# Residual adds free both banks first, background visits go round three times, later DMA landings are assumed, and sample scores take four column tiles at a time

## The chip, the cores and the metric

The kernel runs on one core of a Trainium2 chip. The time is the device time of one execution in microseconds (us). Of before there are three timed runs: 2312.69, 2312.80 and 2317.56 us, median 2312.8 us. The profile is of one more execution, of 2314.36 us, whose span from the first to the last instruction is 2312.2 us.

Engines: PE is TensorE (matmuls), PEld its loading of weights, DVE is VectorE, ACT ScalarE, POOL GpSimd, SP SyncE (which issues most DMAs).

## What is computed

One inference step of a decoder with two layers over a prompt of 512 tokens and a sample group of 8 sequences of 8 tokens, 576 rows in all, with width 2048. Cut to what matters:

```python
def step(x_prompt, x_sample, cache_win_k, cache_win_v, ...):
    # layer 0: attention heads and gated convolution from one projection
    proj = rms_norm(x, g) @ w_in                 # 2048 -> 8 * 1024
    q, k, v, z_a, gate_b, gate_c, h_in, z_b = jnp.split(proj, 8, axis=-1)
    o_a = dilated_attn(q, k, v)                  # sample rows also read the cache, 8 sequences of 2048 keys
    o_b = gate_b * causal_short_conv(gate_c * h_in) * silu(z_b)
    x = x + concat(o_a * silu(z_a), o_b) @ w_out
    # layer 1: diagonal complex SSM, 128 groups of 16 channels and 64 states
    u, z = split(rms_norm(x, g1) @ w_in_c, 2)
    y = gelu(Re(C h(u)) + D * u)
    x = x + (half_glu(y) * silu(z)) @ w_out_c
    return rms_norm(x, g_final), new caches, new states
```

## The kernel before, in words

**Main work.** The projections are cut into 120 jobs: 0 to 23 the heads' q, k and v, 24 to 31 z_a, 32 to 63 the convolution, 64 to 67 the output projection of layer 0 ("wide" jobs of 512 columns), 68 to 99 u and z of layer 1, 100 to 115 the half GLU, 116 to 119 the output projection of layer 1 (wide). Each product is made of three matmuls in a rounded format: `a_hi` by `wh`, `a_lo` by `wh`, `a_hi` by `wl`, where ACT makes `wh` from the loaded weight `w` and DVE makes `wl`, the rest. Accumulators are `mm` tiles of two PSUM banks, of which there are two (four banks); a wide job uses two of them for the 512 prompt rows (column tiles of the result `i` = 0 to 3, tiles 0 and 1 in the first `mm`) and `mms` with `jp` for the 64 sample rows (`i` = 4). `mm_tile` (L595) hands out a new `mm` once all but one of those handed out before have been counted as evacuated in `mmc["ev"]`; before, `finished` (L590) counts when the whole evacuation generator has ended.

**Background work.** Everything else (attention, the loads of the cache, the preparation of layer 1's SSM matrices, the convolution, the scan, residual adds) is written as Python generators, "threads". Each yields `W(engine, tiles, slot=..., flag=...)`: what its next piece waits for. The kernel text is emitted by a planner that keeps an estimated clock for each engine (class `Clock`, L79): `cost` (L151) prices an instruction, `op` adds it to its engine, and a DMA's landing is estimated as the end of its transfer plus a constant (L183). Between the matmuls of the main jobs `between` (L600) calls `step` (L431), which moves every thread once whose wait is over by the estimate (`could`, L405, with a tolerance `EPSN` of 150 ns); evacuations (`cur`) are asked first. So the estimates set the order in which the instructions of each engine stand; at run time real semaphores rule.

**Places that the change touches.** (1) *Sample scores*, `sample_near` (L1428). For each of four pairs of sequences and four blocks of 128 near keys, the keys of one sequence are loaded (`kv`), transposed (`tkn`), copied to `KT` and multiplied: `sps<-KT,qz`, fp32 matmuls with 32 columns of weights, each in a column tile of the array given by `tile_position`. One visit to the scores serves one sequence, in two column tiles. The values follow as `os<-kv,PTs` in four column tiles; the far keys as `kf` on DVE. The kv tiles have 6 buffers, kf 3. (2) *Layer 1's preparation during the heads*: chunks of SSM matrices, whose inputs `E` and `B` are loaded from scratch (one buffer each) when the chunk before has read them; DVE makes `tb`, `X`, `Cs`, and TensorE `gp<-Cs,B`. (3) *Layer 1's scan*: u is written as `uu` to scratch (`u_scr`), loaded back as `U`, and used in `vps<-U`. (4) *Residual adds* `ev_out0` (L1584) and `ev_out1` (L2014): for each bank of an `mm`, DVE adds the residual (`h<-mm,xr` or `Y<-mm,Y`), then ACT squares the sum for the norm. (5) *The tail*, `finish` (L2030), which scales rows by the norm's factor and weights and stores them.

Of the kernel before, what the change touches and what calls it, by code (L numbers as in the profile page):

```python
# [78 lines left out]
class Clock:  # L79
# [71 lines left out]
    def cost(self, eng, op, outs, ins):  # L151
        n = max(int(np.prod(a.shape[1:])) for a in outs[:1] + ins)
        if eng == "PE":
            if op == "transpose":
                return 110.0
            m, k = int(np.prod(ins[0].shape[1:])), int(np.prod(ins[1].shape[1:]))
            if ins[0].dtype == F32R:
                return k / 2.4 + 11 if k < 300 else k / 2.4 + 3
            if m <= 32:
                return max(138.0, 0.55 * k)  # L160
            return 2 * max(109.0, k / 1.2 + 2)
        wide = any(len(a.ap) > 1 and abs(int(a.ap[-1][0])) > 1 for a in outs + ins)
        if eng == "ACT":
            return 175 + 0.89 * n + (190 if len(outs) > 1 else 0)
        if eng == "DVE":
            if op in ("tensor_copy", "tensor_scalar", "memset") and all(a.tensor.name in self.sbuf for a in ins):
                return 150 + n / 1.3
            return 150 + n / (0.6 if wide else 0.96)
        return 200 + (2.15 if op == "tensor_tensor" else 1.0) * n

    def op(self, eng, op, a, k):
        aps = [(n, x) for n, x in list(enumerate(a)) + list(k.items()) if hasattr(x, "tensor")]
        outs = [x for n, x in aps if n in (0, "out", "accum_out")]
        ins = [x for n, x in aps if n not in (0, "out", "accum_out")]
        by = "DMA" if op == "dma_start" else eng
        t = max([self.when(x, False, by) for x in ins] + [self.when(x, True, by) for x in outs])
        if op == "dma_start":
            at = max(self.t[eng], t) + 370
            self.t[eng] = at
            n = int(np.prod(outs[0].shape))  # L180
            run = min(self.packets(x, x.tensor.name in self.row) for x in outs + ins)
            self.dma = max(self.dma, at) + n / run * (5 + 0.2 * run) / 16
            end = max(self.dma, at) + 1900  # L183
        else:
            at = max(self.t[eng], t + 60)
            two = op != "memset" and sum(x.tensor.name in self.sbuf for x in ins) > 1
# [92 lines left out]
def hybrid_step(tc, I, O):  # L279
# [122 lines left out]
    def now():  # L402
        return clk.t["PE"]

    def could(th, deep):  # L405
# [9 lines left out]
        return at <= lim + EPSN  # L415

    def next_evac():
        while evq and not cur:
# [4 lines left out]
    def run(th):  # L423
        if not advance(th):
# [3 lines left out]
            else:  # L428
                bg.remove(th)

    def step():  # L431
        next_evac()
        while cur and could(cur[0], 9000.0):
            run(cur[0])
        for th in list(bg):
            if th in bg and could(th, 3500.0):
                run(th)
                while cur and could(cur[0], 9000.0):
                    run(cur[0])

    def force():
        next_evac()
# [147 lines left out]
    def finished(g, tiles=1, jobs_=1):  # L590
        yield from g
        mmc["ev"] += tiles
        cnt["done"] += jobs_

    def mm_tile():  # L595
        until(lambda: mmc["ev"] > mmc["al"] - 2)
        mmc["al"] += 1
# [12 lines left out]
    def run_wide(n, hook, need):  # L610
        j = jobs[n]
        x, last = wide(j["x"]())
        acc = {}
        evac = lambda part, tiles, done: evq.append(finished(j["evac"](part, j["n"], acc), tiles, done))

        def mms(k, i):
            if k == 0 and i in (0, 2):
# [23 lines left out]
                    mms(k, t)  # L641
            release(n, k)
        i = cnt["i"]
        for t in range(5):
            for k in range(s, 16):
                if (k - s) % 2 == 0:
                    hook(n, k)
# [2 lines left out]
                must(i + k - s)  # L650
                mms(k, t)
            if s < 14:
                evac(t, 1 if t in (1, 3) else 0, 1 if t == 4 else 0)
            elif t in (1, 3, 4):
                evac(t, 1 if t < 4 else 0, 1 if t == 4 else 0)
        for k in range(s, 16):
# [736 lines left out]
                sa["fs"][b // 2] = fs  # L1393

    def sample_out(pr, osb):
        yield W("PE", osb, slot=[bgs()])
# [31 lines left out]
    def sample_near():  # L1428
# [3 lines left out]
        for pr in range(4):  # L1432
# [13 lines left out]
            prev = None  # L1446
            sps = None
            for t in range(4):
                for b2 in range(2):
# [13 lines left out]
                    kts[t, b2] = kk  # L1463
                    at += 1
                    sa["used"] = at
                    if prev:
                        yield W("PE", kts[prev], sa["qz"], slot=[] if sps is not None else [(pm, "bgl", 1)])
                        if sps is None:
                            sps = bgl_tile([P, 4, P], "sps")
                        scores(*prev)  # L1470
                    prev = (t, b2)
            yield W("PE", kts[prev], slot=[bgs(), (pp, "Ss", 1)])
            scores(*prev)
# [107 lines left out]

    h1 = {"x": {}, "xc": 0, "h": {}, "tg": 0, "an": 0, "t": {}, "sn": 0}

    def ev_out0(part, g, acc):  # L1584
        for i in ((0, 1), (2, 3), (4,))[part // 2]:
            n = P if i < 4 else 64
            yield W("DVE", flag=lambda: (g, i) in h1["x"] and (i == 4 or 4 * g + i - 4 * h1["tg"] < 6))
            x = h1["x"].pop((g, i))
            tag = "h" if i < 4 else "hs"
            ps = acc[i, 0]  # L1590
            if i == 4:
                ps = yield from joined(ps)
# [61 lines left out]
    def x_again():  # L1654
        yield W("SP", flag=lambda: "out" in h1)
        k = 0
        for g in range(4):
            for i in range(5):
                yield W("SP", slot=[(EV["p"], "xr", 1)], flag=lambda: k - h1["xc"] < 3)
# [354 lines left out]
    def ev_out1(part, g, acc):  # L2014
        for i in ((0, 1), (2, 3), (4,))[part // 2] if g < 3 else (part,):
            yield W("DVE", flag=lambda: fo.get("h", 0) > g)
            y = fo["Y"][:, i, g * 512:(g + 1) * 512] if i < 4 else fo["Ys"][:, g * 512:(g + 1) * 512]
            n = P if i < 4 else 64
            ps = acc[i, 0]
            if i == 4:  # L2020
                ps = yield from joined(ps)
            yield W("DVE", ps, y)
            add(y, ps, y)
            yield W("ACT", y)
            j = EV["p"].tile([P, 512], F32, name="junk2", tag="junk2", bufs=2)
            act(j[0:n], y, AF.Square, accum_out=ssqa[0:n, 4 * i + g:4 * i + g + 1])
            if g == 3:
                spawn(finish(i), prio=1)

    def finish(i):  # L2030

        n = P if i < 4 else 64
        v, r, w = [fo["s"][0:n, i, k:k + 1] for k in range(3)]
        sq = ssqa[0:n, 4 * i:4 * i + 4]
        yield W("DVE", sq)
        DVE.tensor_reduce(out=w, in_=sq, axis=AX.X, op=ALU.add)
        yield W("ACT", w)
        act(v, w, AF.Identity, scale=1.0 / D, bias=epst[0:n])
        act(r, v, AF.Sqrt)
        yield W("DVE", r)  # L2040
        newton(v, r, w)
        yield W("DVE", flag=lambda: "gl" in fo)
# [158 lines left out]
```

## Time and profile before

| | us |
|---|---|
| median of three runs | 2312.8 |
| profiled execution, its own time | 2314.36 |
| its span | 2312.2 |
| TensorE busy | 2207.9 |
| VectorE busy | 1261.2 |
| ScalarE busy | 689.9 |

TensorE's granted clock has a mean of 0.98 of full speed. All helper calls are recorded under L215, so groups are told apart by the names of their tiles. In actual time the heads run from about 17 to 440 us, z_a to 580, the convolution to 1140, the output projection of layer 0 to 1360, u and z to 1885, the half GLU to 2090, the last output projection to 2301. Times below are us from the start of the span; in brackets stands how long the engine was idle before, and what released it. "x16" counts instruction records; an fp32 matmul leaves two.

### The profile page before, as it was taken

What the parts mean: (1) busy time and instruction counts of PE and PEld (TensorE: products, weight loads), DVE (VectorE), ACT (ScalarE), POOL (GpSimd) and SP (SyncE); (2) the same over time, 40 slices, a digit from 0 to 9 for tenths busy, and PEclk for the clock granted to TensorE, in tenths of its full rate; (3) what the DMA queues carried; (4) which work ended last, traced back from release to release, by engine and by line L of the source; (5) the groups of instructions that cost most, each with busy time, mean ns of one, the idle gap of its engine ahead of it and who ended that gap; (6) DMA issues with size and microseconds to landing.
All of it is one profiled execution on the core that took longest, in us unless ns stands there. A gap on an engine that the chain in (4) does not pass through costs nothing.

```text
span 2312.2 us, 38336 instructions
## 1 busy us (share of the span) xinstructions
PE 2207.9 (95%) x15581; PEld 2035.5 (88%) x15581; DVE 1261.2 (55%) x2360; ACT 689.9 (30%) x1400; POOL 14.2 (1%) x52
## 2 busy tenths in 40 slices
PE   5998999999899999999999999999999999999997
PEld 5998898889879789897977779999999999998786
DVE  3666876765656754233433334888895444443223
ACT  4442333332212222121332332222223333232221
POOL 0000000000000000000000000000000000000000
PEclk8999999999999999999999999999999999999999
DMA  5456776659999995847565435466546643338322
GB/s 163 105 137 177 191 200 167 188 172 252 226 262 258 222 289 136 267 115 201 173 188 171 139 110 155 127 183 196 153 153 174 192 122 104 107 106 202 101 64 82
DMA packets 423740, 388.98 MB, mean 168 GB/s; under 512 B 34964, under 2 KB 350204, under 8 KB 422796
## 3 DMA queue, kind: packets, MB, share of 16 engines
q1 hardware_dynamic: 371048, 342.34, 54.8%
q10 hardware_dynamic: 52452, 44.19, 6.1%
q8 instruction: 122, 2.00, 0.4%
q14 instruction: 54, 0.44, 0.1%
q0 software_dynamic: 64, 0.02, 0.0%
HBM read 330.40 MB, written 64.46 MB: 171 GB/s over the span
## 4 chain that ended last, share of the span: by engine, by line
PE 71%; DMA 13%; DVE 10%; issue 2%; ACT 2%; SPq 2%; ACTq 0%; DVEq 0%
PE mm L215 59%; DMA B<-b_scr 3%; DVE m L215 3%; PE mms L215 2%; DMA kv<-cache_win_v 2%; PE yps L215 2%; DVE wl L215 2%; PE os L215 2%; SPq L215 2%; DMA cs_scr<-Cs 1%; DMA kf<-cache_win_k 1%; PE vps L215 1%; PE tkn L215 1%; PE sps L215 1%; DMA w<-w_in_ab 1%
## 5 line engine op out<-in xcount | busy, mean ns | idle before, releaser
L215 DVE TENSOR_TENSOR wl<-w,wh 128x512 fp32r<-128x512 f32 x576 | 394.2, 689 | 577.4 <-ACT wh L215 553.9
L215 PE MATMUL mm<-a_hi,wh 128*128 128x288 f32 x3072 | 700.8, 310 | 8.1 <-ACT a_hi L215 8.1
L215 PE MATMUL mm<-a_lo,wh 128*128 128x288 f32 x3072 | 664.2, 298 | 6.1 <-DVE a_lo L215 6.1
L215 PE MATMUL mm<-a_hi,wl 128*128 128x288 f32 x3072 | 664.5, 298 | 1.5 <-DVE wl L215 1.5
L215 ACT ACTIVATE wh<-w 128x512 fp32r<-128x512 f32 x576 | 357.9, 627 | 655.7 <-PE mm L215 318.2
L215 PEld LDWEIGHTS mm<-a_hi,wh 128*128 128x128 f32 x3072 | 497.6, 192 | 61.5 <-issue 38.6
L215 PEld LDWEIGHTS mm<-a_lo,wh 128*128 128x128 f32 x3072 | 501.3, 192 | 7.3 <-DVE a_lo L215 7.3
L215 PEld LDWEIGHTS mm<-a_hi,wl 128*128 128x128 f32 x3072 | 500.1, 191 | 1.7 <-DVE wl L215 1.7
L215 PE MATMUL mm<-y_hi,wh 128*128 128x288 f32 x512 | 109.7, 296 | 0.0
L215 PE MATMUL mm<-y_lo,wh 128*128 128x288 f32 x512 | 109.7, 296 | 0.0
L215 PE MATMUL mm<-y_hi,wl 128*128 128x288 f32 x512 | 109.5, 296 | 0.0
L215 PE MATMUL mm<-wh,o_hi 128*128 128x512 f32 x256 | 101.4, 396 | 5.2 <-DVE h L215 5.2
L215 PE MATMUL mm<-wh,a_hi 128*128 128x512 f32 x256 | 99.9, 390 | 1.6 <-DVE Y L215 1.6
L215 PE MATMUL mm<-wl,o_hi 128*128 128x512 f32 x256 | 99.9, 390 | 0.0
L215 PE MATMUL mm<-wh,o_lo 128*128 128x512 f32 x256 | 99.8, 390 | 0.0
L215 PE MATMUL mm<-wh,a_lo 128*128 128x512 f32 x256 | 99.6, 389 | 0.0
L215 PE MATMUL mm<-wl,a_hi 128*128 128x512 f32 x256 | 99.6, 389 | 0.0
L215 PEld LDWEIGHTS mm<-y_hi,wh 128*128 128x128 f32 x512 | 82.5, 189 | 0.0
L215 PEld LDWEIGHTS mm<-y_lo,wh 128*128 128x128 f32 x512 | 82.5, 189 | 0.0
L215 PEld LDWEIGHTS mm<-y_hi,wl 128*128 128x128 f32 x512 | 82.5, 189 | 0.0
L215 DVE TENSOR_TENSOR kf<-kf,qr 128x1024 f32<-128x1024 f32 x48 | 58.6, 1221 | 37.6 <-DMA kf<-cache_win_k 37.4
L215 DVE TENSOR_TENSOR m<-HV,AT 64x256 f32<-64x256 f32 (+5 forms) x120 | 67.7, 564 | 5.6 <-ACT HV L215 3.2
(287 smaller groups left out, 2357.8 us busy)
## 6 DMA issues: line engine op xcount, KB each, us to landing
w<-w_in_ab SPq DMA_DIRECT2D x128, 512.0 KB
kv<-cache_win_v SPq DMA_DIRECT2D x80, 512.0 KB
w<-w_in_c SPq DMA_DIRECT2D x64, 512.0 KB
kf<-cache_win_k SPq DMA_DIRECT2D x48, 512.0 KB
kv<-cache_win_k SPq DMA_DIRECT2D x32, 512.0 KB
w<-w_out_ab SPq DMA_DIRECT2D x32, 512.0 KB
w<-w_glu SPq DMA_DIRECT2D x32, 512.0 KB
w<-w_out_c SPq DMA_DIRECT2D x32, 512.0 KB
```

The costliest lines, as they stand in the source:

```text
L215: r = f(*a, **k)
```

## The change

Six edits. (a) `Clock.cost` prices the rounded matmuls by one formula (the same for 288 columns, 227.1 ns in place of 216.3 for 512). (b) A DMA's landing is assumed 3200 ns after its transfer in place of 1900. (c) `step` goes round the threads up to three times as long as something moved, and evacuations get a tolerance of 400 ns. (d) `scores` takes both sequences of a block in one visit, alternating over four column tiles. (e) `ev_out0` and `ev_out1` do both adds of a bank pair, count the banks as free (`freed`), and leave the squares to later; `xr` gets four buffers in place of three. (f) In the last wide job the sample's tile comes first; the norm's weights are multiplied in as soon as a slice is added (`times_g`), and `finish` then scales a whole row on DVE (1152 columns) and ACT (896) and issues its stores from SP and ACT in turn. `sample_out` also waits for job 32.

```diff
-                return k / 2.4 + 11 if k < 300 else k / 2.4 + 3
+                return k / 2.333 + 7.6
...
-            end = max(self.dma, at) + 1900
+            end = max(self.dma, at) + 3200
...
-        for th in list(bg):
-            if th in bg and could(th, 3500.0):
-                run(th)
-                while cur and could(cur[0], 9000.0):
-                    run(cur[0])
+        evacs()
+        for _ in range(3):
+            again = False
+            for th in list(bg):
+                if th in bg and could(th, 3500.0):
+                    run(th)
+                    again = True
+                    evacs()
+            if not again:
+                return
...
+    def freed(part, tiles):
+        mmc["ev"] += tiles if part < 4 else 0
...
-        for t in range(5):
+        for t in range(5) if s == 14 else (4, 0, 1, 2, 3):
...
-            def scores(t, b2):
-                kk = kts.pop((t, b2))
+            def scores(t):
+                kk = [kts.pop((t, b2)) for b2 in range(2)]
                 for h4 in range(4):
-                    for hg in range(2):
-                        r0 = b2 * 64 + hg * 32
-                        PE.matmul(sps[r0:r0 + 32, t, :], sa["qz"][:, b2, hg, h4, :],
-                                  kk[:, hg * 4 + h4, :], start=h4 == 0, stop=h4 == 3,
-                                  tile_position=(0, r0))
+                    for b2 in range(2):
+                        for hg in range(2):
+                            r0 = b2 * 64 + hg * 32
+                            PE.matmul(sps[r0:r0 + 32, t, :], sa["qz"][:, b2, hg, h4, :],
+                                      kk[b2][:, hg * 4 + h4, :], start=h4 == 0, stop=h4 == 3,
+                                      tile_position=(0, r0))
...
             add(h, ps, x)
             h1["h"][g, i] = h
+            got.append((i, n, h, x))
+        freed(part, tiles)
+        for i, n, h, x in got:
             yield W("ACT", h)
...
-                x = EV["p"].tile([P if i < 4 else 64, 512], F32, name="xr", tag="xr", bufs=3)
+                x = EV["p"].tile([P if i < 4 else 64, 512], F32, name="xr", tag="xr", bufs=4)
...
+    def times_g(i, g, n, y):
+        yield W("DVE", y, flag=lambda: "gl" in fo)
+        mul(y, y, fo["g"][0:n, g * 512:(g + 1) * 512])
+        fo["gd", i] = fo.get(("gd", i), 0) + 1
...
-        for c in range(2):
-            cols = slice(1024 * c, 1024 * c + 1024)
-            y = fo["Y"][:, i, cols] if i < 4 else fo["Ys"][:, cols]
-            yield W("DVE", y, fo["g"])
-            stt(y, y, r, fo["g"][0:n, cols], ALU.mult, ALU.mult)
-            yield W("SP", y)
-            for p0, p1, rows in pieces(i, yp, ys):
-                SP.dma_start(out=rows[:, cols], in_=y[p0:p1])
+        DVE.tensor_scalar(out=y[:, 0:1152], in0=y[:, 0:1152], scalar1=r, scalar2=None, op0=ALU.mult)
+        act(y[:, 1152:], y[:, 1152:], scale=r)
+        yield W("SP", y)
+        for k, (p0, p1, rows) in enumerate(pieces(i, yp, ys)):
+            (ACT if k % 2 else SP).dma_start(out=rows, in_=y[p0:p1])
```

The order of TensorE's instructions around the sample scores of before (`sps` are scores, `tkn` transposed keys; a name's number tells tiles apart, and `KT` with one number is one sequence's keys):

```order
L215 MATMUL sps_6036<-KT_6160,qz_5859 32x128 x8
L215 MATMUL tkn_6269<-ident_74,kv_5987 128x128 x4
L215 MATMUL tkn_6275<-ident_74,kv_5987 128x128 x4
L215 MATMUL sps_6036<-KT_6225,qz_5859 32x128 x8
L215 MATMUL tkn_6294<-ident_74,kv_6005 128x128 x4
L215 MATMUL tkn_6300<-ident_74,kv_6005 128x128 x4
L215 MATMUL sps_6036<-KT_6268,qz_5859 32x128 x8
```

Eight matmuls read one `KT`; the next sequence's keys are scored in a run of their own. The same place after the change:

```order
L215 MATMUL mm_5516<-a_hi_99,wl_5462 128x288 x2
L215 MATMUL sps_5592<-KT_5532,qz_5387 32x128 x2
L215 MATMUL sps_5592<-KT_5565,qz_5387 32x128 x2
L215 MATMUL sps_5592<-KT_5532,qz_5387 32x128 x2
L215 MATMUL sps_5592<-KT_5565,qz_5387 32x128 x2
L215 MATMUL sps_5592<-KT_5532,qz_5387 32x128 x2
L215 MATMUL sps_5592<-KT_5565,qz_5387 32x128 x2
L215 MATMUL sps_5592<-KT_5532,qz_5387 32x128 x2
L215 MATMUL sps_5592<-KT_5565,qz_5387 32x128 x2
L215 MATMUL tkn_5612<-ident_74,kv_5434 128x128 x4
```

Now sixteen matmuls stand in one run and alternate between the keys of two sequences, so over four column tiles. The 32 runs of eight have become 16 runs of sixteen.

The order of VectorE's instructions at the first boundary between two wide jobs of layer 0's output projection, before (`h` is the residual sum, `mm` with one number one pair of banks):

```order
L215 TENSOR_TENSOR h_12274<-mm_11928,xr_12203 128x512
L215 TENSOR_TENSOR h_12284<-mm_11928,xr_12217 128x512
L215 TENSOR_TENSOR h_12296<-mm_11951,xr_12228 128x512
L215 TENSOR_TENSOR wl_12319<-w_12170,wh_12306 128x512
L215 TENSOR_TENSOR wl_12321<-w_12170,wh_12310 128x512
L215 TENSOR_TENSOR h_12323<-mm_11951,xr_12288 128x512
L215 TENSOR_TENSOR h_12340<-jp_12338,xr_12300 64x512
```

And after:

```order
L215 TENSOR_TENSOR h_12264<-mm_11958,xr_11992 128x512
L215 TENSOR_TENSOR h_12266<-mm_11958,xr_11994 128x512
L215 TENSOR_TENSOR h_12286<-mm_11973,xr_12002 128x512
L215 TENSOR_TENSOR h_12288<-mm_11973,xr_12004 128x512
L215 TENSOR_TENSOR h_12326<-jp_12324,xr_12278 64x512
L215 TENSOR_TENSOR wl_12335<-w_12173,wh_12300 128x512
L215 TENSOR_TENSOR wl_12337<-w_12173,wh_12306 128x512
```

The two `wl` that stood between the adds of the second pair of banks now stand behind all adds of the job.

## Rows read from the trace of the kernel before

**Rows 1.** Page, part 1: busy us (share of the span), x instructions.

```profile
PE 2207.9 (95%) x15581; PEld 2035.5 (88%) x15581; DVE 1261.2 (55%) x2360; ACT 689.9 (30%) x1400; POOL 14.2 (1%) x52
```

**Rows 2.** Windows (from:to, length): busy PE, PEld, DVE, ACT, POOL; PEclk, DMA share, GB/s.

```profile
165.00:450.00 285.00, 262.29 (x1996) 247.65 (x1995) 208.31 (x438) 99.78 (x232) 0.00 (x0) 0.95 0.69 183
...
527.00:866.00 339.00, 322.74 (x2554) 288.08 (x2553) 212.58 (x287) 75.25 (x141) 3.08 (x16) 0.97 1.02 254
866.00:1140.00 274.00, 273.36 (x2212) 245.22 (x2211) 104.43 (x195) 67.75 (x131) 1.74 (x8) 1.00 0.64 178
...
1361.00:1760.00 399.00, 382.47 (x2924) 378.31 (x2924) 310.95 (x662) 109.04 (x248) 3.43 (x7) 0.98 0.55 160
```

**Rows 3.** TensorE's waits: who waited <- for what: total us, times, longest us.

```profile
PE gp L215 <- DVE Cs L215: 21.8, 17, 2.8
PE vps L215 <- DMA U<-u_scr: 9.7, 4, 4.0
...
PE os L215 <- DMA kv<-cache_win_v: 8.7, 5, 3.2
PE mm L215 <- ACT a_hi L215: 8.1, 2, 6.9
PE mm L215 <- DVE a_lo L215: 6.1, 3, 5.6
PE tf L215 <- DVE E L215: 5.8, 1, 5.8
PE mm L215 <- DVE h L215: 5.2, 3, 1.7
```

**Rows 4.** Windows behind a gp wait and behind a U wait.

```profile
184.20:191.00 6.80, 4.72 (x23) 4.24 (x22) 3.05 (x8) 0.73 (x3) 0.00 (x0) 0.50 0.88 243
1655.30:1662.10 6.80, 5.34 (x23) 5.38 (x24) 5.55 (x10) 2.13 (x5) 0.00 (x0) 0.50 0.71 202
```

**Rows 5.** Timeline of TensorE at a score visit: start, us, instruction.

```profile
711.50 0.42 PE L215 MATMUL mm<-a_lo,wh 128*128 128x288 f32 x2
711.76 0.43 PE L215 MATMUL mm<-a_hi,wl 128*128 128x288 f32 x2
712.12 1.07 PE L215 MATMUL sps<-KT,qz 128*32 128x128 f32 x16
...
713.49 0.42 PE L215 MATMUL mm<-a_lo,wh 128*128 128x288 f32 x2
```

**Rows 6.** Timeline of TensorE at a visit to the sample's values.

```profile
646.69 0.42 PE L215 MATMUL mm<-a_hi,wl 128*128 128x288 f32 x2
647.04 1.06 PE L215 MATMUL os<-kv,PTs 128*32 128x512 f32 x8
...
648.40 0.42 PE L215 MATMUL mm<-a_lo,wh 128*128 128x288 f32 x2
```

**Rows 7.** Chain of waits in the heads: start, us from issue to landing.

```profile
185.59 12.29 DMA B<-b_scr
203.11 11.37 DMA B<-b_scr
```

**Rows 8.** Timeline of VectorE around the same loads.

```profile
181.89 0.69 DVE L215 TENSOR_TENSOR X<-X,tb 128x512 f32<-128x512 f32 x1
197.98 0.69 DVE L215 TENSOR_TENSOR tb<-E,B 128x512 f32<-128x512 f32 x1 [4.68 <-DMA B<-b_scr]
...
202.48 0.69 DVE L215 TENSOR_TENSOR X<-X,tb 128x512 f32<-128x512 f32 x1
```

**Rows 9.** Timeline at the first boundary of the output projection.

```profile
1191.91 1.29 DVE L215 TENSOR_TENSOR wl<-w,wh 128x512 fp32r<-128x512 f32 x2 [1.31 <-ACT wh L215]
1193.12 0.68 DVE L215 TENSOR_TENSOR h<-mm,xr 128x512 f32<-128x512 f32 x1
...
1193.86 0.50 PE L215 MATMUL mm<-wh,o_hi 128*128 128x512 f32 x1 [1.73 <-DVE h L215]
```

**Rows 10.** Timeline of TensorE's last instruction, in the tail.

```profile
2300.05 1.07 PE L215 MATMUL jp<-js,rstd 128*64 128x512 f32 x2 [0.69 <-ACT js L215]
```

More of the change, by code (lines that the diff above doesn't have):

```diff
@@ L403, in now, with could @@
         return clk.t["PE"]
-    def could(th, deep):
+    def could(th, deep, eps=EPSN):
         w = th["w"]
@@ L414, in could @@
             lim = max(lim, clk.t[w[0]])
-        return at <= lim + EPSN
+        return at <= lim + eps
     def next_evac():
@@ L429, in run, with evacs @@
                 bg.remove(th)
+    def evacs():
+        next_evac()
+        while cur and could(cur[0], 9000.0, 400.0):
+            run(cur[0])
     def step():
-        next_evac()
-        while cur and could(cur[0], 9000.0):
-            run(cur[0])
-        for th in list(bg):
-            if th in bg and could(th, 3500.0):
-                run(th)
-                while cur and could(cur[0], 9000.0):
-                    run(cur[0])
+        evacs()
[8 more added lines that the diff above has]
+                return
     def force():
@@ L613, in run_wide @@
         acc = {}
-        evac = lambda part, tiles, done: evq.append(finished(j["evac"](part, j["n"], acc), tiles, done))
+        evac = lambda part, tiles, done: evq.append(finished(j["evac"](part, j["n"], acc, tiles), 0, done))
         def mms(k, i):
@@ L652, in run_wide @@
             if s < 14:
-                evac(t, 1 if t in (1, 3) else 0, 1 if t == 4 else 0)
+                evac(t, 1 if t in (1, 3) else 0, 1 if t == 3 else 0)
             elif t in (1, 3, 4):
@@ L1395, in sample_out @@
     def sample_out(pr, osb):
-        yield W("PE", osb, slot=[bgs()])
+        yield W("PE", osb, slot=[bgs()], flag=lambda: cnt["done"] >= 32)
         tp = bg_tile([P, 4, 4, 4, NS], "to")
@@ L1435, in sample_near @@
             kts = {}
-            def scores(t, b2):
-                kk = kts.pop((t, b2))
+            def scores(t):
+                kk = [kts.pop((t, b2)) for b2 in range(2)]
                 for h4 in range(4):
-                    for hg in range(2):
-                        r0 = b2 * 64 + hg * 32
-                        PE.matmul(sps[r0:r0 + 32, t, :], sa["qz"][:, b2, hg, h4, :],
-                                  kk[:, hg * 4 + h4, :], start=h4 == 0, stop=h4 == 3,
-                                  tile_position=(0, r0))
-            prev = None
+                    for b2 in range(2):
[4 more added lines that the diff above has]
+                                      tile_position=(0, r0))
             sps = None
@@ L1465, in sample_near @@
                     sa["used"] = at
[L1466 to L1473, printed above, removed]
+                yield W("PE", kts[t, 0], kts[t, 1], sa["qz"], slot=[] if sps is not None else [(pm, "bgl", 1)])
+                if sps is None:
+                    sps = bgl_tile([P, 4, P], "sps")
+                scores(t)
+            yield W("PE", slot=[bgs(), (pp, "Ss", 1)])
             S = pp.tile([P, 1344], F32, name="Ss", tag="Ss")
@@ L1582, in hybrid_step, with ev_out0 @@
     h1 = {"x": {}, "xc": 0, "h": {}, "tg": 0, "an": 0, "t": {}, "sn": 0}
[L1584 to L1587, printed above, removed]
+    def ev_out0(part, g, acc, tiles):
+        mine = ((0, 1), (2, 3), (4,))[part // 2]
+        yield W("DVE", flag=lambda: all((g, i) in h1["x"] for i in mine) and (part == 4 or 4 * g + part - 4 * h1["tg"] < 6))
+        got = []
+        for i in mine:
+            n, tag = (P, "h") if i < 4 else (64, "hs")
             x = h1["x"].pop((g, i))
-            tag = "h" if i < 4 else "hs"
             ps = acc[i, 0]
@@ L1658, in x_again @@
             for i in range(5):
-                yield W("SP", slot=[(EV["p"], "xr", 1)], flag=lambda: k - h1["xc"] < 3)
-                x = EV["p"].tile([P if i < 4 else 64, 512], F32, name="xr", tag="xr", bufs=3)
+                yield W("SP", slot=[(EV["p"], "xr", 1)], flag=lambda: k - h1["xc"] < 4)
+                x = EV["p"].tile([P if i < 4 else 64, 512], F32, name="xr", tag="xr", bufs=4)
                 src = I["x_prompt"][0][i * P:(i + 1) * P] if i < 4 else xsam
@@ L2012, in h_again, with ev_out1 @@
         fo["gl"] = True
[L2014 to L2017, printed above, removed]
+    def ev_out1(part, g, acc, tiles):
+        cols = slice(g * 512, (g + 1) * 512)
+        mine = ((0, 1), (2, 3), (4,))[part // 2] if g < 3 else (part,)
+        yield W("DVE", flag=lambda: fo.get("h", 0) > g)
+        got = []
+        for i in mine:
             n = P if i < 4 else 64
+            y = fo["Y"][:, i, cols] if i < 4 else fo["Ys"][:, cols]
             ps = acc[i, 0]
@@ L2023, in ev_out1 @@
             add(y, ps, y)
+            got.append((i, n, y))
+        freed(part, tiles)
+        for i, n, y in got:
             yield W("ACT", y)
@@ L2028, in ev_out1 @@
                 spawn(finish(i), prio=1)
+            else:
+                spawn(times_g(i, g, n, y), prio=2)
+    def times_g(i, g, n, y):
+        yield W("DVE", y, flag=lambda: "gl" in fo)
+        mul(y, y, fo["g"][0:n, g * 512:(g + 1) * 512])
+        fo["gd", i] = fo.get(("gd", i), 0) + 1
     def finish(i):
@@ L2034, in finish @@
         sq = ssqa[0:n, 4 * i:4 * i + 4]
+        y = fo["Y"][:, i, :] if i < 4 else fo["Ys"]
         yield W("DVE", sq)
         DVE.tensor_reduce(out=w, in_=sq, axis=AX.X, op=ALU.add)
-        yield W("ACT", w)
-        act(v, w, AF.Identity, scale=1.0 / D, bias=epst[0:n])
+        DVE.tensor_scalar(out=v, in0=w, scalar1=1.0 / D, scalar2=EPS, op0=ALU.mult, op1=ALU.add)
         act(r, v, AF.Sqrt)
-        yield W("DVE", r)
+        mul(y[:, 1536:], y[:, 1536:], fo["g"][0:n, 1536:])
+        yield W("DVE", r, flag=lambda: fo.get(("gd", i), 0) == 3)
         newton(v, r, w)
-        yield W("DVE", flag=lambda: "gl" in fo)
         yp, ys = O["y_prompt"][0], O["y_sample"].rearrange("b s f -> (b s) f")
-        for c in range(2):
-            cols = slice(1024 * c, 1024 * c + 1024)
-            y = fo["Y"][:, i, cols] if i < 4 else fo["Ys"][:, cols]
-            yield W("DVE", y, fo["g"])
-            stt(y, y, r, fo["g"][0:n, cols], ALU.mult, ALU.mult)
-            yield W("SP", y)
-            for p0, p1, rows in pieces(i, yp, ys):
-                SP.dma_start(out=rows[:, cols], in_=y[p0:p1])
+        DVE.tensor_scalar(out=y[:, 0:1152], in0=y[:, 0:1152], scalar1=r, scalar2=None, op0=ALU.mult)
[3 more added lines that the diff above has]
+            (ACT if k % 2 else SP).dma_start(out=rows, in_=y[p0:p1])
     def pieces(i, prompt, sample):
```

## Prediction

> **What bounds the kernel now.** I read the engine totals first: TensorE is busy for 95% of the span [rows 1], so time can only come from TensorE's own work or from its waits. Next the windows by stage [rows 2], in which the reader should compare TensorE's busy time with the length of the window, then the granted clock and the DMA share. From 866 us to 1140 us TensorE is busy throughout at full clock. In the heads (165 to 450 us) it lacks 22.7 us and the clock averages 0.95. In the stretch from 527 to 866 us, where the old cache is read, it lacks 16.3 us, the DMA engines are full (share 1.02) and move 254 GB/s. In layer 1's scan (1361 to 1760 us) it lacks 16.5 us. Third, the table of TensorE's waits [rows 3]: gp waits for Cs (heads), vps for the load of U (scan), os and tf (the cache stretch), h (the output projection), and two long waits at the start, for a_hi and a_lo. Each longer wait is followed by a stretch at half clock (1.2 GHz): after one gp wait 6.8 us at 0.50, after one U wait 6.8 us at 0.50 [rows 4]. So a wait of 3 to 4 us costs about as much again, since 6.8 us at half clock do the work of 3.4.
>
> **TensorE's work: -23.1 us.** A visit is a break in the main matmuls for background matmuls. A pair of main matmuls starts 0.26 us after the one before it. Around a score visit of 16 records (8 matmuls of two passes) the starts at 711.76 and 713.49 are 1.73 us apart and hold two pairs, so the visit costs 1.73 - 0.52 = 1.21 us [rows 5]. The built order of before has 32 such visits. After, 16 visits hold 32 records each, on four column tiles in place of two. What would such a visit cost? The nearest row is the os visit: 8 records of 512 columns on four column tiles, 4096 columns, and by its starts at 646.69 and 648.40 it costs 1.71 - 0.52 = 1.19 us [rows 6], although it streams twice the columns of the score visit of before (16 records of 128 columns, 2048). The new score visit streams 4096 columns on four tiles as well, so I take 1.2 us. That saves 16 x 1.2 = 19.2 us. The bound on the other side is that no more than two tiles run at once: then the second half of each visit adds its streaming time again. Visits of both kinds cost 1.2 us at twice the tiles and twice the columns, so I split 1.2 us into about 0.34 us of entering and leaving and 0.86 us of streaming; the new visit would cost 2.06 us and the saving shrink to 5.5 us.
>
> The Trainium skill, "TensorE: Matmul & The Clock Gate", Part 3, section "Measured speedup vs the span model", gives 2.38 times for three column tiles and 3.07 times for four row tiles, not 3 and 4. By the second figure the new visit would stream 0.86 x 4/3.07 = 1.12 us and the saving be about 15 us (an estimate); the os row, with four tiles as quick per tile as the scores with two, disagrees.
>
> The rounds of the planner join visits: counted over the built order, visits fall from 363 to 262. Most of those hold transposes only, whose joining saves next to nothing. The os visits go from 44 to 32, at 0.34 us each 4.0 us. The sum is 19.2 + 4.0 = 23.1 us (rounded).
>
> **The cache stretch: +28 us.** The built order is drawn together. Priced with the paces above, TensorE's work from the first kv load to the last kf consumed goes from 303.5 us to 261.1 us, for the same 86.5 MB. In the trace 339 us x 254 GB/s = 86.1 MB [rows 2] took 339 us with the engines full. To move it in 261 us would take 332 GB/s. If the DMA engines need what they needed, the stretch takes 320 us (if the 5% or so in which some engine idled is used too) to 341 us. So its excess over TensorE's work, 35 us before (339 less 303.5), becomes 59 to 80 us: 24 to 45 us are given back. I take 28, near the lower end, since the loads start earlier, while the za jobs ask little of the DMA, and part of the added lag lies in buffers. The saving of the scores is therefore mostly hidden: the scores lie in just this stretch. Nothing is given back later, as the stretch behind it runs with a DMA share of 0.64 [rows 2].
>
> **The heads: +9 us.** Each of 16 chunks loads E and B into a single buffer. The issue at 185.59 landed 12.29 us later, the one at 203.11 after 11.37 us [rows 7]. From the last X of one chunk (ends 182.58) to that landing are 15.3 us, and DVE then stands on tb for 4.68 us [rows 8]; for the next, 203.17 to 214.48, 11.3 us. The order gives these loads as much TensorE work as stands between X and the next tb: a mean of 14.2 us before and 12.8 after (least 8.7). Sixteen times 1.4 us is 22 us of longer waits on DVE, behind which stand the wl halves and Cs. Against it, gp stands further behind the last Cs: 4.9 us of work in place of 3.7, 16 x 1.2 = 19 us, which would swallow most of gp's 21.8 us [rows 3]. The net is +3, and some half-clock stretches more make it +9. Ends: -5 (gp's waits go) and +30 (none of the longer lead helps).
>
> **Layer 1's scan: -13 us.** The four vps waits are 9.7 us [rows 3]. A mean clock of 0.98 over the 399 us [rows 2] is some 16 us at half clock, 8 us lost. The lead from uu to vps grows from 11.0 to 15.7 us before to 15.0 to 20.9 after at all waiting places but one, where it grows by 0.2 only. Three waits go (about 7.2 us) and most of the lost clock (5.8 us). Ends: -8 and -15.
>
> **The boundaries of the output projection: -5.2 us.** At three boundaries TensorE waits 1.73 us for h: DVE does two wl (1.29 us) between the adds of the two halves of a tile [rows 9]. The order now puts both adds of a bank pair in front of the wl. Nothing else is late: with both adds done the next tile starts. ACT's squares move behind, where they have slack. If the adds are late by one wl instead, 0.65 us each stay.
>
> **Start and tail: -2 and -1 us.** The waits for a_hi and a_lo (6.9 and 5.6 us, [rows 3]) change their order: two more x tiles are rounded ahead of the third w split, yet two squares now lie between; I take 2 us, ends 0 and -5. In the last job the sample's tile comes first, so js and jp (0.69 us of wait, 1.07 us of work, [rows 10]) leave the end; the last prompt tile's scaling, DVE on 1152 columns and ACT on 896, stands there instead, and its row of output is 1 MB and not half of it. Ends: -3 and +1. Multiplying by the norm's weights earlier lies under TensorE's work. Output issues shared between SP and ACT cost nothing, since both have slack there.
>
> **Sum.** -23.1 + 28 + 9 - 13 - 5.2 - 2 - 1 = -7.3 us. The profiled execution took 2314.4 us (span 2312.2), 1.6 us above the median of 2312.8. Against its own time the sum gives 2307.1, against the median 2305.5 us. The change is large in what it moves and small in its net.
>
> **Rivals.**
> (1) *The buffers carry the cache stretch.* Six kv and three kf buffers, and loads that begin 46 us of work earlier, spread the bytes, and the +28 vanishes: 2305.5 - 28 = 2277 us. For it: the DMA share is at 0.64 behind and 0.69 ahead of the stretch [rows 2]. Against it: share 1.02 within, and tf and os already wait there [rows 3]. The Trainium skill, "DMA: Bandwidth & Descriptors", section "Specifications", gives about 358 GB/s of HBM for a core; by that 86.5 MB need 242 us, less than the 261 us, and this rival would hold. The row's 254 GB/s at a full share disagrees for these packets.
> (2) *The heads turn late (slower).* If tb waits longer in each chunk, DVE's queue (wl, Cs behind it) is late as well, and the longer gp lead is no relief, since Cs moves with tb: the whole 22 us come, and, since a wait costs about as much again at half clock [rows 4], some 18 us with them. That is +40 in place of +9: 2336 us; it decides when the lead falls below the 11.3 to 15.3 us that a load needs, and in the order it is below 11.3 for about a third of the chunks.
> (3) *The four tiles don't run at once*, or the lagging cache stretch eats all of it: 0 to 14 us less of a gain, 2306 to 2319 us. Against it: the os row.
>
> **How the numbers follow.** The forecast's own case (2296 to 2318) has a chance of 0.45, rival 1 0.22, rival 2 0.20, rival 3 0.13. A measurement here can tell about 0.2%, 4.6 us, from no change: faster is below 2308.2, slower above 2317.4. Faster: 0.27 of the first case, 0.21 of rival 1, 0.02 of rival 3: 0.50. Same: 0.13 of the first, 0.01 and 0.07 of the others: 0.21. Slower: 0.05, 0.20 and 0.04: 0.29. The range of 8 in 10 goes from 2278 (rival 1) to 2333 (most of rival 2).
>
> **What would show it.** Right: score visits of 32 records at about 1.2 us; TensorE busy falling by some 20 us and more; waits on kv, kf and tf in the cache stretch growing by some 15 us and more at a DMA share near 1; gp's waits smaller but tb's longer; no h wait of 1.73 us; one vps wait at most. Wrong: the cache stretch ending with its work at a share well under 1 (rival 1), gp and wl waits in every chunk with a clock under 0.93 in the heads (rival 2), or score visits of 2 us (rival 3).

## The result: slower, 2348.8 us against 2312.7

The changed kernel took 2348.84 us (median of four runs, 2346.7 to 2350.4) against 2312.74 us for the kernel before on the same chip: a ratio of 1.0159, 95% interval 1.0129 to 1.0190. The forecast of 2305.5 us and the range up to 2333 both miss it, and the sign is wrong. The profiled execution has a span of 2348.5 us, 36.3 us more than the 2312.2 us of before.

The page of the changed kernel, part 1 (columns as in [rows 1]):

```profile
PE 2206.3 (94%) x15581; PEld 2034.7 (87%) x15581; DVE 1264.8 (54%) x2380; ACT 695.8 (30%) x1400; POOL 13.5 (1%) x52
```

TensorE's waits of the changed kernel (columns as in [rows 3]):

```profile
PE tq L215 <- ACT XY L215: 20.0, 3, 7.0
PE mm L215 <- DVE wl L215: 12.6, 4, 8.2
...
PE tf L215 <- DVE E L215: 11.2, 3, 5.8
PE pt L215 <- ACT S L215: 10.9, 6, 3.1
PE os L215 <- DMA kv<-cache_win_v: 10.5, 10, 2.8
PE s L215 <- DVE S L215: 8.6, 2, 4.6
PE yps L215 <- issue: 6.6, 2, 4.3
PE sps L215 <- DVE KT L215: 6.2, 5, 4.2
...
PE gp L215 <- DVE Cs L215: 4.2, 2, 2.2
...
PE vps L215 <- DMA U<-u_scr: 2.6, 3, 2.2
```

Compare with [rows 3]: gp fell from 21.8 to 4.2 us, vps from 9.7 to 2.6, the three waits for h are gone. In their place stands a wait that the table of before doesn't have at all, tq for ScalarE's XY (20.0 us in three waits), then waits of the heads for ScalarE's S and VectorE's S, of the cache stretch for wl, tf, os and KT, and of the scan for yps. TensorE idles 142 us in the span, 104 us before.

To see where, I priced each kernel's built order with the paces of [rows 5, 6], which gives TensorE's work up to every main matmul, and took it from the time at which the trace shows that matmul. What is left is the lag; the table has how much it grows in each stage (us, of one profiled execution each). The sum of a row's stages and its work is its span. "Start" holds all that lies ahead of main matmul 700, "rest" all behind 9300, the tail in it. The stages end at main matmul 700, 2420 (heads, and the start of z_a), 5000 (cache stretch), 7030 (output projection of layer 0), 9300 (scan).

| kernel | span | work | start | heads | cache stretch | output proj. | scan | rest |
|---|---|---|---|---|---|---|---|---|
| before | 2312.2 | 2133.9 | 37.2 | 48.1 | 33.2 | 11.4 | 29.2 | 19.2 |
| changed | 2348.5 | 2110.8 | 34.6 | 70.9 | 80.9 | 4.4 | 26.4 | 20.5 |
| difference | +36.3 | -23.1 | -2.6 | +22.8 | +47.7 | -7.0 | -2.8 | +1.3 |
| forecast | -7.3 | -23.1 | -2 | +9 | +28 | -5.2 | -13 | -1 |

Three terms failed: the cache stretch, the heads and the scan.

### The profile page after: what moved, and what is told of

Read it like the earlier page. It is cut to its first block, busy times and chain, and to the rows that moved or that the text cites. A ratio compares the mean times of both kernels' runs of the same rounds, so it can differ in the third digit from the quotient of the medians.

```text
span 2348.5 us, 38368 instructions
## 1 busy us (share of the span) xinstructions
PE 2206.3 (94%) x15581; PEld 2034.7 (87%) x15581; DVE 1264.8 (54%) x2380; ACT 695.8 (30%) x1400; POOL 13.5 (1%) x52
## 4 chain that ended last, share of the span: by engine, by line
PE 70%; DMA 15%; DVE 9%; ACT 3%; issue 2%; SPq 1%; ACTq 0%; DVEq 0%
PE mm L215 59%; DMA kv<-cache_win_v 4%; DMA kf<-cache_win_k 3%; PE mms L215 3%; DVE m L215 2%; PE yps L215 2%; DMA B<-b_scr 2%; DMA out_win_k_p<-ktok 1%; PE os L215 1%; DVE wl L215 1%; DMA oa<-oa_scr 1%; SPq L215 1%; DMA w<-w_in_ab 1%; PE vps L215 1%; PE tkn L215 1%
```

## The experiments

Twelve kernels were run; ratios are against the kernel before, run beside each, with 95% intervals.

**1. Is the cache stretch held by the rate of its loads?** Far keys and values are 8 of every 16 rows of the cache; here they are 128 consecutive rows, in the changed kernel and in the one before.

```diff
-        return c[b, t * 256:(t + 1) * 256].rearrange("(j r) f -> j r f", r=16)[:, 0:8, :]
+        return c[b, t * P:(t + 1) * P, :]
```

> The changed kernel with the far keys and values read as 128 consecutive cache rows in place of 8 of every 16 (other rows of the cache, so the sample's attention is of other keys; same bytes, same instructions in the same order on every engine). Theory A, the cache stretch is held by the rate of the far loads: the kf waits of VectorE (79.3 us) at least halve, the stretch shrinks by 25 to 50 us, the kernel gets 2300 to 2325 us. Theory B, the loads are merely issued too late or stand behind other work in the queues: kf waits stay and the time stays at 2340 to 2350 us.

> The same replacement of the far rows in the kernel before (the sample's attention is of other keys). Theory A: before asks less of the DMA engines in the stretch, so it gains less than the changed kernel does, 8 to 20 us (2293 to 2305 us). Theory B: no change, 2308 to 2316 us.

The changed kernel came to 2285.8 us, ratio 0.986 (0.982 to 0.990), where 1.016 was measured with the real rows: some 69 us gained, more than theory A asked for. Before came to 2286.7 us, 0.986 (0.982 to 0.990): 32 us, where theory A had written 8 to 20. VectorE's waits for kf, first of the changed kernel:

```profile
DVE kf L215 <- DMA kf<-cache_win_k: 79.3, 24, 15.5
```

and in the same order of instructions with consecutive rows:

```profile
DVE kf L215 <- DMA kf<-cache_win_k: 17.7, 4, 12.6
```

The window from the first kv load to the last kf consumed shows the cause (columns as in [rows 2]; the last three numbers are granted clock, DMA share, GB/s). Before:

```profile
528.41:872.87 344.46, 328.20 (x2603) 293.18 (x2603) 218.58 (x294) 74.99 (x140) 3.08 (x16) 0.97 1.02 254
```

The changed kernel:

```profile
503.20:843.50 340.30, 300.05 (x2446) 262.65 (x2444) 209.68 (x272) 69.57 (x128) 5.05 (x24) 0.93 1.02 261
```

The changed kernel with consecutive rows:

```profile
498.93:782.27 283.34, 277.48 (x2446) 249.04 (x2444) 208.35 (x272) 70.25 (x128) 5.91 (x24) 0.99 0.94 313
```

Before with consecutive rows:

```profile
523.92:838.56 314.64, 313.86 (x2573) 284.71 (x2572) 218.26 (x294) 74.88 (x139) 4.24 (x16) 1.00 0.85 279
```

Read the second number, the length, and the last two. With the real rows the stretch lasts 344 us before and 340 us after, at a full share and 254 and 261 GB/s, although the order after holds 261.1 us of TensorE's work in it and the one before 303.5. The rate hangs on the rows read: the same order with other rows moves 313 GB/s and the stretch is 57 us shorter. Nearly all of the gain lies there: the two profiled spans of the changed kernel differ by 64.9 us, and 62.6 of them stand between main matmul 2420 and 5000 (526.3 and 463.7 us). Theory B, late or badly queued loads, is out. With consecutive rows, too, the changed kernel is no faster than before (0.986 both); its heads still wait 19.8 us for tq.

**2. Is the scores' saving hidden?** The score visits of before put back into the changed kernel, and the new ones alone put into the kernel before. The edit of the second, as far as the visit goes:

```diff
                 for h4 in range(4):
-                    for hg in range(2):
+                    for b2 in range(2):
+                        for hg in range(2):
```

> The changed kernel with the score visits of before (two column tiles, one sequence a visit); its order holds 18.7 us more of TensorE's work than the changed one, 13.7 of it in the cache stretch. Theory A, the stretch is set by the loads, so work of TensorE added in it is hidden: ratio to before 1.010 to 1.022 (the changed kernel: 1.016). Theory G, the scores' work lies on the path: 1.022 to 1.028.

> The kernel before with the new score visit alone (four column tiles, both sequences at once); its order holds 17.7 us less of TensorE's work, 21 us less in the cache stretch. Theory A: the loads set the end of the stretch and give nearly all of it back, ratio to before 0.995 to 1.001. Theory G: the work saved is time saved, 0.991 to 0.993.

Undone: 1.0157 (1.0121 to 1.0193), the same as the changed kernel's 1.0159, with 18.7 us more work. Alone: 0.9978 (0.9961 to 0.9995), 5 us gained of 17.7 us removed; the lag of its cache stretch grew from 33.2 to 51.4 us. Its window, in the same columns:

```profile
521.85:865.98 344.13, 316.97 (x2519) 282.30 (x2518) 214.97 (x289) 72.74 (x136) 3.30 (x16) 0.96 1.01 250
```

344.1 us again: most of what leaves TensorE in this stretch comes back as waits. Both runs fit theory A.

That doesn't make the length a constant. Over the twelve kernels that read the real rows it goes from 325 to 365 us, with the engines at a share of 0.99 to 1.03 in each. The two ends are the changed kernel with its key store moved (experiment 3), in the very same order of TensorE's instructions, and the kernel of experiment 5:

```profile
497.60:822.15 324.55, 292.98 (x2446) 257.52 (x2444) 209.38 (x272) 69.56 (x128) 4.45 (x24) 0.95 1.03 271
502.00:866.83 364.83, 332.62 (x2672) 296.64 (x2670) 219.29 (x296) 77.71 (x144) 2.31 (x16) 0.96 0.99 243
```

What moves the rate between 243 and 271 GB/s is open.

**3. What holds ScalarE in the heads?** In the trace of the changed kernel, ScalarE's timeline (ACTq is its queue, which issues DMAs between its instructions):

```profile
178.07 0.46 ACTq L215 DMA_DIRECT2D out_win_k_p<-ktok  x1
178.63 11.25 ACTq L215 DMA_DIRECT2D gz_scr<-gsb  x4
189.93 0.40 ACT L215 ACTIVATE S<-S,st 128x128 f32<-128x128 f32 x1 [11.89 <-DMA gz_scr<-gsb]
...
190.33 0.35 ACT L215 ACTIVATE XY<-tx,sgn 128x128 f32<-128x128 f32 x1
...
190.90 0.64 PE L215 MATMUL tq<-ident,qk 128*64 128x128 f32 x2 [7.05 <-ACT XY L215]
```

Four stores of gsb, 32 KB each, take 11.25 us to issue, and softmax (S), XY and then TensorE's tq wait for that. The same happens at 303.1 and 425.6 us (some 11 us each), and for 4.3 to 4.5 us at 258.2 and 382.8. Such holds are no novelty of the change: before has them too, the longest at 364.97 (8.91 us), 416.48 (6.19) and 456.02 (8.61). But no wait for tq follows them there; what is new is what the order puts behind them. The built order with its waits names the reason:

```text
L215 DMA out_win_k_p<-ktok 128x4x128 [waits DMAHW4_49,Activation_49]
L215 DMA gz_scr<-gsb 16x4x128 [waits DMAHW6_49,DVE_49]
L215 DMA gz_scr<-gsb 16x4x128 [waits DMAHW1_49]
L215 DMA gz_scr<-gsb 16x4x128 [waits DMAHW2_49]
L215 DMA gz_scr<-gsb 16x4x128 [waits DMAHW4_49]
```

In the order the waits run through eight such names, DMAHW0 to DMAHW7: a transfer takes one of eight completion semaphores in turn, and its issue waits until the transfer that had the same one before has landed. The key store's turn is DMAHW4, and the fourth gsb store waits on DMAHW4 again, so on the key store issued just before. The chain of waits has that store's landing:

```profile
178.07 11.48 DMA out_win_k_p<-ktok
```

It ends at 189.55 us, the issue at 189.88. But the key store is only the last of three such waits. The trace has the issues one by one (SPq is SyncE's queue):

```profile
176.33 0.60 SPq L215 DMA_DIRECT2D E<-e_scr  x1
177.06 0.34 ACTq L215 DMA_DIRECT2D bx_scr<-X  x1
...
183.95 0.34 ACTq L215 DMA_DIRECT2D gz_scr<-gsb  x1
186.35 0.31 ACTq L215 DMA_DIRECT2D gz_scr<-gsb  x1
189.57 0.31 ACTq L215 DMA_DIRECT2D gz_scr<-gsb  x1
```

In the order, the transfers eight places ahead of the second, third and fourth gsb store are the load of E, the store of X and the key store; by the trace they land at 183.92, 186.33 and 189.55 us, and each gsb store starts 0.02 to 0.03 us behind. So the load of E holds the queue first, and the key store only for the last 3.2 us.

Two experiments move one kind of store to GpSimd, which has a queue of its own, and leave the order of all else as it is. First the key store:

```diff
-        ACT.dma_start(out=kout[:, h, :].rearrange("(i p) d -> p i d", p=P), in_=kt_)
+        kd = dict(out=kout[:, h, :].rearrange("(i p) d -> p i d", p=P), in_=kt_)
+        POOL._raw.dma_start(**kd)
+        clk.op("ACT", "dma_start", (), kd)
```

> The changed kernel with the heads' key stores (out_win_k_p<-ktok) issued by GpSimd in place of ScalarE; the order of all other instructions is the same. Theory C, in the heads ScalarE's queue is held for 11 us each time by the issue of a gz_scr store that must wait for the key store issued eight transfers before: the three tq waits (20.0 us) go, with some half clock behind them, 2318 to 2332 us. Theory D, the heads are held by the E and B loads and ScalarE only shows it: less than 5 us, 2344 to 2350 us.

It measured 2337.9 us, ratio 1.0090 (1.0056 to 1.0123): about 16 us gained of the 17 to 31 expected. The trace tells why so little: the turn of the semaphores has moved by one transfer, the hold still stands behind the load of E and the store of X, and only the key store's part is gone.

```profile
174.20 0.33 ACTq L215 DMA_DIRECT2D bx_scr<-X  x1
...
175.13 8.91 ACTq L215 DMA_DIRECT2D gz_scr<-gsb  x4
...
185.05 0.64 PE L215 MATMUL tq<-ident,qk 128*64 128x128 f32 x2 [4.34 <-ACT XY L215]
```

The heads gained next to nothing in this profile: from main matmul 700 to 2420 it shows 349.3 us, against 351.7 in the changed kernel. It is of the fastest of seven executions (2325.7 us), and what it gained lies in the cache stretch (324.55 us, above). So this run doesn't tell theory C from theory D. The next one moves the four gsb stores themselves:

```diff
-                    ACT.dma_start(
+                    kd = dict(
                         out=gz_scr[(c - 1) * CH:(c + 1) * CH].rearrange("(q gi) k j -> gi k q j", gi=4)[gi][:, :, 112:240],
                         in_=gsb[32 * gi:32 * gi + GC])
+                    POOL._raw.dma_start(**kd)
+                    clk.op("ACT", "dma_start", (), kd)
```

> The changed kernel with the four gz_scr stores of each chunk pair issued by GpSimd in place of ScalarE; the order of all else is the same. With the key store moved (the run before) the issue still held ScalarE for 8.9 us, behind an earlier store. Theory C, the held queue of ScalarE is a cost of its own in the heads: the tq waits (20.0 us in the changed kernel, 10.7 with the key store moved) fall below 5 us, ratio to before 1.001 to 1.010. Theory D, the E and B loads hold the heads: tq waits are replaced by others, 1.012 to 1.018.

2307.4 us, ratio 0.9962 (0.9946 to 0.9978): 45 us less than the changed kernel, more than expected, from moving 32 small stores. The tq waits are gone from the table, and the same place reads:

```profile
176.61 0.46 ACTq L215 DMA_DIRECT2D out_win_k_p<-ktok  x1
177.07 2.05 POOL L1276 DMA_DIRECT2D gz_scr<-gsb  x4 [124.19 <-DVE wl L215]
178.28 0.40 ACT L215 ACTIVATE S<-S,st 128x128 f32<-128x128 f32 x1 [1.70 <-DVE st L215]
...
181.48 0.38 PE L215 MATMUL tq<-ident,qk 128*64 128x128 f32 x2
```

S follows at 178.28 in place of 189.93. The heads' lag falls from 70.9 to 37.0 us, below the 48.1 of before; from main matmul 700 to 2420 the trace now shows 317.9 us in place of 351.7. The held queue was thus worth 34 us in the heads, and theory D, by which the move gains little, is out. What else the two profiles differ by lies in the start (3) and in the cache stretch (6), and in the latter kernels of the same order differ by more than that (526.3 us here, 508.9 with the key store moved).

**4. Which edit made it?** The rounds and the landing, each undone and each alone.

```diff
-        for _ in range(3):
+        for _ in range(1):
```

> The changed kernel with one round through the background threads in place of three. Counted over its order the cache stretch holds 297 us of TensorE's work for 86.6 MB (changed kernel 261, before 303.5). Theory A: the stretch's excess over TensorE's work falls back to near that of before, 30 to 45 us are saved against 5 us more of TensorE's work: 2308 to 2325 us. Theory E, another edit (later landings, the scores' visit) makes the loss: 2338 to 2350 us.

> The changed kernel with landings assumed 1900 ns after a transfer as before; three rounds stay. Theory H, three rounds are what draws the stretch together and puts the stores in a row on ScalarE, with either landing: ratio to before 1.012 to 1.025. Theory I, the later landing makes the loss by its order: below 1.005.

> The changed kernel with one round and landings of 1900 ns, so that of the change the scores, the two banks, the tail and the prices of matmuls are left. Theory H: near the kernel with one round and 3200 (0.988), 0.984 to 0.996. If the later landing is what helps the heads and the scan there (10 us and more of waits on E, B and U), 0.996 to 1.002.

> The kernel before with landings assumed 3200 ns after the transfer and nothing else changed. Theory J, later landings alone move the readers of E, B and U behind their loads, and gp's, tb's and vps' waits shrink: ratio to before 0.988 to 0.996. Theory K, they help only together with the other edits: 0.997 to 1.003.

> The kernel before with three rounds (and the condition of sample_out on job 32, which they need) and nothing else changed; its cache stretch asks for 324 GB/s in place of 285. Theory H, the rounds alone make the loss: ratio to before 1.008 to 1.022. Rival, the loss needs the shorter score visits or the later landings too: 0.997 to 1.005.

| rounds | landing | other edits | ratio (95%) | heads | cache stretch | scan | rest |
|---|---|---|---|---|---|---|---|
| 1 | 1900 | no (before) | 1 | 48.1 | 33.2 | 29.2 | 19.2 |
| 1 | 3200 | no | 0.9911 (0.9880-0.9942) | 26.8 | 37.7 | 20.8 | 19.2 |
| 3 | 1900 | no | 1.0250 (1.0214-1.0285) | 54.8 | 67.1 | 46.3 | 23.7 |
| 1 | 1900 | yes | 0.9969 (0.9953-0.9985) | 50.7 | 48.6 | 24.8 | 28.9 |
| 1 | 3200 | yes | 0.9878 (0.9839-0.9916) | 28.2 | 54.4 | 17.6 | 29.5 |
| 3 | 1900 | yes | 1.0150 (1.0111-1.0189) | 48.3 | 83.9 | 50.2 | 26.9 |
| 3 | 3200 | yes (changed) | 1.0159 (1.0129-1.0190) | 70.9 | 80.9 | 26.4 | 20.5 |

The last four columns are the growth of the lag in us, of one profiled execution each, as in the first table. Three rounds with 3200 and without the other edits were not run. Three rounds cost in every pairing (0.025, 0.018 and 0.028 of the ratio, from top to bottom), and 26 to 35 us of it each time in the cache stretch. The later landing gains 0.009 with one round (some 22 us in the heads, 7 to 8 in the scan) and nothing with three, where its 24 us in the scan are paid for by 23 us in the heads: TensorE's waits for tq are 20.0 us in that pairing, 4.1 us with three rounds and 1900, and none with one round. The one-round kernel gained more than I had written (0.988, 2290 us), because I had counted the stretch and not the heads. The rounds alone came out slower than my upper end (1.022). The kernel with one round and 1900 fell just outside the first band, in the second: the later landing is worth 0.009 there, which I had kept for the case of the longer waits. With one round and the other edits the rest grows by 10 us (a wait of 6.0 us for Y in the last projection is part of it); why is open.

**5. A version that beats both.** One round, and the gsb stores issued by GpSimd.

> The same move in the kernel with one round, where ScalarE's queue was held for 1.9 us at most. Theory C: nothing to free, ratio to before 0.984 to 0.990 (0.988 without the move). If it gains over 10 us, the stores cost more than the held queue shows.

2281.9 us, ratio 0.9848 (0.9824 to 0.9873), within the expectation: 33 us faster than before. Its interval overlaps that of the one-round kernel (0.9839 to 0.9916), so that the move gains something there is not shown. My premise for it was wrong besides: the one-round kernel does have one hold of 8.05 us, at 407.85 us, not 1.9 at most.

## Why the prediction was wrong, point by point

Three steps failed. In the heads, the issues on ScalarE's queue were priced at nothing and cost 34 us. For the cache stretch, the lower end of a bracket was taken (+28) and +38 to +48 came. In the scan, the wait of yps for HV was left at nothing, and of -13 only -2.8 came.

**TensorE's work, -23.1 us: right as a count, wrong as time.** The new score visit costs what the os row said. TensorE's timeline of the changed kernel:

```profile
521.11 0.42 PE L215 MATMUL mm<-a_hi,wl 128*128 128x288 f32 x2
521.46 1.08 PE L215 MATMUL sps<-KT,qz 128*32 128x128 f32 x32
522.47 1.09 PE L215 MATMUL tkn<-ident,kv 128*128 128x128 f32 x8
523.32 0.51 PE L215 MATMUL mm<-a_hi,wh 128*128 128x288 f32 x2
523.67 0.42 PE L215 MATMUL mm<-a_lo,wh 128*128 128x288 f32 x2
```

The starts at 521.11 and 523.67 are 2.56 us apart; less two pairs (0.52) and the eight transposes (0.85, from 522.47 to 523.32) 1.19 us are left. Rival 3 in its first form, tiles that don't run at once, is out. The Trainium skill, "TensorE: Matmul & The Clock Gate", Part 3, section "Measured speedup vs the span model", gives 3.07 times for four row tiles. By that figure a visit would cost 1.46 us (an estimate, 0.34 + 1.12 as in the prediction), and the trace has 1.19 us for these four column tiles. The rival's second form, a stretch that eats the saving, is what experiment 2 shows. My sign for the evidence failed too: TensorE's busy time fell by 1.6 us and not by 20. More of the span runs at half clock: from the granted clock of the stages some 13 us more of the work's time is lost than before, which makes busy time longer. The rest of that difference, about 9 us, is not explained.

**The cache stretch, +28 forecast, +47.7 measured: the mechanism right, the size wrong.** The step that failed is the choice inside a bracket that held the answer: 320 to 341 us for the stretch, of which I took the lower end with the reason that earlier loads and buffers would absorb part. The stretch lasted 340.3 us, the upper end: in this profile nothing was absorbed. No row stood behind the lower end. That the upper end was met is in part luck, as the same order took 324.6 us with the key store moved and 334.8 with the gsb stores moved. From the window alone the difference is (340.3 - 261.1) - (344.5 - 303.5) = 38 us. The other 10 us of the stage are within what the two ways of counting differ by: for before the window alone gives 41 us, more than the 33.2 of the whole stage that holds it. Rival 1 is out with its ground: at a full share the engines move 243 to 271 GB/s of these rows, and it needed 332. The Trainium skill, "DMA: Bandwidth & Descriptors", section "Specifications", has about 358 GB/s of HBM for a core. No stretch measured here came to it, not even with consecutive rows (313 at a share of 0.94).

**The heads, +9 forecast, +22.8 measured: the wrong engine.** The step was right to ask who waits for E and B, but its 22 us of longer waits on VectorE didn't come: the waits for tb fell from 28.7 to 18.5 us, where I had them longer. gp's waits went as counted (21.8 to 4.2). With the stores moved the heads lag 37.0 us, 11 less than before; how much of that is gp's longer lead is not shown, as before has holds of its own and was not run without them, and with three rounds and 1900 gp's waits are 4.2 us as well and the heads lag 48.3. What I didn't do is walk ScalarE's queue. The order put the four gsb stores straight behind the load of E, the store of X and the key store, and of moved steps I had priced only the instructions on TensorE and VectorE. It cost 34 us. Rival 2's time (2336 us) is the nearest of all, but its mechanism is not what ran: the heads turned late by ScalarE's issues and not by tb.

**The scan, -13 forecast, -2.8 measured: a wait replaced.** The vps waits went as counted (9.7 to 2.6 us). In their place stand two waits of yps, 6.6 us, one of them here (TensorE and VectorE of the changed kernel):

```profile
1617.20 0.56 DVE L215 TENSOR_TENSOR HV<-HV,m 128x224 f32<-128x224 f32 x1
...
1617.86 0.41 PE L215 MATMUL yps<-HV,css 128*128 128x72 f32 x2 [4.34 <-issue]
```

yps starts 0.1 us after VectorE has finished HV, so the "issue" of this row is a wait for VectorE. The half clock behind the waits stayed (mean clock 0.98 in both). The step counted leads from uu to vps and none from HV to yps. With one round the same edits give 17.6 us of lag and not 26.4: -11.6 against before, close to the -13, with 2.4 us of waits for yps. So the three rounds took it back. That they do it by asking for HV earlier, on a stretch in which VectorE is busy for 79% of the time (311 of 395 us), fits the rows above but was not tested.

**What held.** The boundaries of the output projection: forecast -5.2, measured -7.0, no wait for h left. The start: -2 forecast, -2.6 measured. The tail: -1 forecast; the table's +1.3 is of the whole rest. From the start of the last main matmul to the end of the span the trace shows 13.2 us before and 12.8 after, so the tail itself gained 0.4 us.

The sum of the misses is 19.7 (stretch) + 13.8 (heads) + 10.2 (scan) + 2.3 (rest) - 0.6 - 1.8 = 43.6 us, the distance from -7.3 to +36.3.

## What to carry to other kernels

Find the stretch in which the DMA engines are full, and measure how long its bytes take. TensorE's work inside it gains little when it is removed (5 us of 17.7 here) and costs nothing measurable when it is put back (18.7 us, 1.0157 and 1.0159), so a scheduler that draws such a stretch together with less other work inside mostly moves work out of its cover. When a schedule changes, walk the queues of all engines that issue DMAs, the issues included: a store of 32 KB held ScalarE until an unrelated transfer eight places ahead had landed, since both share a completion semaphore. And where a bracket's one end is the rate seen in the trace and the other needs a better one, don't lean to the better one without a row for it.

## What I had not expected of the hardware

The rate depends on which rows are read, at equal bytes and row length: 8 of every 16 rows of 4 KB give 243 to 271 GB/s at a full share of the engines, 128 consecutive rows for the same loads 313 GB/s at 0.94 (the loads of near rows and of weights are among both numbers). Why is open. And five holds of one engine's queue, three of them of 11 us, cost 34 us in the heads (without them the kernel goes from 1.016 to 0.996), since the instructions behind them feed TensorE, and the clock falls with it: from 150 to 505 us it is 0.94 in the changed kernel and 0.98 with the stores moved.
